# Column sums by whole dense passes, and a fill whose steps stand wider apart, in a one-core decoder layer

## The chip, the cores and the metric

The kernel runs on one core of one Trainium2 chip. The metric is the time of one execution on the device, in microseconds (us), and lower is better. A core has five engines that run side by side, each through its own queue in order: TensorE (PE, matmuls), VectorE (DVE), ScalarE (ACT), GpSimd (POOL) and SyncE (SP), which here mostly issues DMAs. Engines wait for each other by semaphores.

## The reference

One layer of a decoder trunk over 1024 tokens of width 2048, all in float32:

```python
h = rmsnorm(h_res, g_pre)
u = h @ w_in                       # one projection, columns cut into groups
log_a = log_sigmoid(g_lr @ w_a2 + b_a) / GLA_TAU
o_gla = rmsnorm(gla_chunked(gq, gk, gv, log_a), g_head) * silu(g_gate)
o_sb  = stick_breaking(sq, sk, sv) * silu(s_gate)
mix   = concat([o_gla, o_sb]) @ w_out
h_res = h_res + rmsnorm(mix, g_post)
gate  = sigmoid(h_res @ w_g + b_g)
out   = h_res + gate * (p @ w_p)
```

`gla_chunked` is gated linear attention with 4 heads of key width 128. Inside a chunk its score between tokens i and j <= i is the sum over the 128 channels of `q_i * k_j * exp(b_i - b_j)`, where `b` is the running sum of `log_a`. On the diagonal i = j the exponential is 1, so the score is the sum over channels of `q_i * k_i`. `stick_breaking` has 8 heads and plays no part in the change, save that it uses the same buffers afterwards.

## The kernel before, in words

Activations lie with channels on the 128 partitions and tokens along the free dimension, in two halves of 512 tokens. A float32 matrix product is made of three passes: both factors are split into a high part of reduced precision (F32R) and the rest, and `hi*hi`, `lo*hi` and `hi*lo` are accumulated. `split(hi, lo, src)` is one ACT copy and one DVE subtraction.

**First part, the projection and both attentions.** `dense` walks over the projection's units of 128 columns. After every six matmuls (one of 16 slices of the width, both halves, three passes) it calls `step()`, which gives a turn to each of the queues `urgent`, `beside` and `jobs`. Attention is written as generators in `jobs`: a `yield 1` gives the turn back, so that attention's instructions are traced between the dense matmuls. With `RATE_GLA` 1.0 one GLA job gets one turn per step.

`gla` handles a head, half by half. It makes `b` from the gate's matmul `lg` (L414), then `qe` and `ke`, turns the keys by a DMA transpose (`turn_by_dma`, L356 to L362: ACT separates the 16-bit halves into a buffer `mid`, SP issues the transposing DMA into a second one, and DVE joins the halves later, for the keys at L506 in `join_keys`), waits `W0` turns, and then works through seven levels of distance, `LEVELS`. At levels 64 to 2, `factors` makes exponentials and products on DVE and ACT in a buffer `X` (two of them), `level` (L461) makes two matmuls into a PSUM buffer `z` (two of them), and `put` (L455) copies the masked result into the scores `sc` by a `copy_predicated` on DVE. `W1` turns lie ahead of the first level and `W2[i]` ahead of level i.

Two contributions need no matmul between tokens but a sum over channels, that is over partitions: the diagonal (`prep_diag`, `put_diag`) and the last level, distance 1 (`prep_one`, `put_one`). Both go through `by_rows` (L468): four groups of float32 matmuls with a stationary operand of ones, 32 columns wide, each placed in its own quarter of the PE's columns (`tile_position`). So each group writes only those 32 rows of the result that are needed, and four masked copies of 32 rows each follow (L485, L500). The product of the diagonal takes a buffer `E` (two of them), traced right before the first `factors`; `put_diag` stands with the first level.

The values of a head are turned in the same way by `turn` (L364): buffers `X` and `E`, `VW` turns of waiting, then a DVE copy.

**Second part, three products of a recursive form.** The gate, output and last projections are each done by a scheme with sums of quarter matrices, which saves one product in eight. Each stage runs over 8 column blocks j. In most stages a j has one product (24 matmuls); in three stages it has two products, with three weight loads, two weight sums and two splits per j. Sets of activations, split in four pairs of tiles 1024 wide, lie in three slots. While a stage runs, the set for a later stage is made by `fill` (L975) in a free slot: loads into staging buffers (`staged`, three `ar` and one `cw` in turn), for some sets a sum on DVE (`join`), then `to_slot`, which splits. `fill` is a job as well; `RATE_BG` is 0.5, so it gets one turn for every two `step()` calls, and `product` calls `step()` once for every three matmuls, so a stage with 16 products offers 64 turns. After a stage `drain` traces what is left. The change touches the fills that run in two of the long stages: `S3` of the output projection (L1152; two loads and one difference per pair) and `S4` of the last gate (L1341; one load and two sums per pair).

**What sets the order.** The program is traced in the order above, each instruction with its place as its priority; `tc.high_priority(offset=n)` moves it n places ahead. When the kernel is built, a scheduler makes each engine's queue from this: the first in priority among the instructions that it expects to be ready. Weight loads and splits (`ahead`, 700) and the sums behind a product (`soon`, 300) are moved ahead this way; `put_one` has 800 on its copies. On the chip the queues are then fixed.

Of the kernel before, what the change touches and what calls it, by code (L numbers as in the profile page):

```python
# [12 lines left out]
F32R = mybir.dt.float32r  # L13
# [33 lines left out]
RATE_GLA = 1.0  # L47
W0, W1, W2, W4 = 2, 6, (2, 3, 3, 3, 2, 3), 2
RATE_SB = 0.9
W3 = 4  # L50
V_MID, V_END, VW = ("X", "X"), ("E", "E"), 3
L1, L2, PERIOD = 8, 8, 5
# [10 lines left out]
def layer(ctx, tc, xT, w_in, w_gate, w_lr, w_a2, b_a, g_pre, g_head, w_out, g_post,  # L63
# [40 lines left out]
    def f(t):  # L104
        return t.bitcast(F32)
# [196 lines left out]
    with tc.tile_pool(name="att", bufs=1, reuse_waits="tile") as ap:  # L302
# [53 lines left out]
        def turn_by_dma(src, n, mid, tag):  # L356
            pl = at(mid, (P, 2 * n), U16)
            A.activation(pl.rearrange("p (two n) -> p two n", two=2),  # L358
                         src.bitcast(U16)[:, :2 * n].rearrange("p (n two) -> p two n", two=2), AF.Copy)
            tt = at(tag, (P, 2 * n), U16)  # L360
            nc.sync.dma_start(tt.rearrange("p (c t) -> p c t", t=P), pl, transpose=True)
            return tt.rearrange("p (two c t) -> p two c t", two=2, t=P)  # L362

        def turn(vt, dst, parts):  # L364
            w = turn_by_dma(vt, HT, V_MID[parts - 1], V_END[parts - 1])
            for _ in range(VW):
                yield 1
            full = dst if parts == 1 else at("o")
            V.tensor_copy(full.bitcast(U16).rearrange("p (c t two) -> p two c t", c=4, two=2), w)
            if parts == 2:  # L370
                split(*dst, full)
            yield 1
# [31 lines left out]
        def gla(h, kp, qp, vp):  # L404
# [6 lines left out]
            for hf in HALVES:  # L411
# [26 lines left out]
                turned_keys = turn_by_dma(ke, HT, "s", "E")  # L438
                G.tensor_tensor(qe, qe, q, op=ALU.mult)
                for _ in range(W0):  # L440
                    yield 1
# [25 lines left out]

                def by_rows(e, n, m):  # L468
                    z = ps("z")
                    rows = [slice(32 * g, 32 * g + 32) for g in range(4)]  # L470
                    for g, r in enumerate(rows):
                        PE.matmul(z[r, :4 * n].rearrange("p (c t) -> p c t", c=4), f(ones_r)[:, :32],
                                  view(e, n * g, (m, 4), (1, n)), start=True, stop=True,
                                  tile_position=(0, 32 * g))
                    return [(r, z[r, :4 * n]) for r in rows]

                def prep_diag():
                    e = at("E")
                    V.tensor_tensor(e, k, q, op=ALU.mult)
                    return e  # L480

                def put_diag(e):
                    for g, (r, z) in enumerate(by_rows(e, 32, P)):
                        m = mask_s[r, 7 * QT + 32 * g:7 * QT + 32 * g + 32].rearrange("p (c t) -> p c t", c=1)
                        V.copy_predicated(view(sc[r], 32 * g, (P, 4), (1, 32)), m.to_broadcast([32, 4, 32]),  # L485
                                          z.rearrange("p (c t) -> p c t", c=4))

                def prep_one():
                    e = at("E", (P, QT))
                    e4 = e.rearrange("p (s n h) -> p s n h", s=2, h=1)  # L490
                    V.tensor_tensor(e4, queries(b, 1), keys(b, 1), op=ALU.subtract)
                    A.activation(e, e, AF.Exp, scale=1.0 / TAU)
                    times(e4, e4, keys(k, 1))
                    times(e4, e4, queries(q, 1))
                    return e

                def put_one(e):
                    for g, (r, z) in enumerate(by_rows(e, 16, 64)):
                        with tc.high_priority(offset=800):
                            V.copy_predicated(view(sc[r], 32 * g + 1, (QT - 1, 2), (P, 2), (2, 16)),  # L500
                                              view(mask_s[r], 6 * QT + 16 * g, (P, 2), (64, 2), (1, 16)),
                                              z.rearrange("p (s c t) -> p s c t", s=2, c=2))

# [18 lines left out]

                diag, xs = prep_diag(), factors(LEVELS[0])
                for _ in range(W1):
                    yield 1
                for i in range(6):
# [3 lines left out]
                    if i == 0:  # L530
                        ket = join_keys()
                        put_diag(diag)
                    level(i, x)
# [370 lines left out]
    if True:  # L904
# [69 lines left out]

        def fill(name, slot, load, join=None):  # L975
            pairs = []
            ready = load(0)
            yield 1
            for i in range(4):
                now, ready = ready, load(i + 1) if i < 3 else None  # L980
                yield 1
                if join:
                    now = join(*now)
                    yield 1
                pairs.append(to_slot(slot, i, now))
                yield 1
# [164 lines left out]

        job(fill("S3", 0, *both(og_d[1], og_d[0], sub)))  # L1152
        for j in range(8):
# [186 lines left out]
        st_v = state("l")  # L1340
        job(fill("S4", 2, make_4, join_4))  # L1341
        for j in range(8):
# [111 lines left out]
```

## Time and profile before

| | us |
|---|---|
| median of 3 runs | 2054.58 |
| lowest and highest | 2049.41, 2055.2 |
| the profiled execution | 2058.89 |
| its span, first to last instruction | 2057.2 |

Over the span the DMA engines moved 173 GB/s on the mean; the page's 40 slices show 82 to 108 GB/s in most of the first half and 200 to 330 in most of the second. The granted clock of PE stands at 0.9 or more of full speed in each slice. The output stage with two products per j runs from 1433.6 to 1523.7 us of the span, the gate stage with two products per j from 1797.4 to 1888.5; the eight GLA passes lie between about 117 and 548.

To read the rows that follow: a row in order of time has the start, the duration, the engine, the line, the operation with `output<-inputs` by tile names, the shape, and a count where like instructions in a row are put together; brackets give idle time before it and what ended it. Matmuls are pipelined, so a duration is longer than the distance to the next start; what a matmul costs PE is that distance. A row of a list of waits has the waiting instruction, its releaser, then total us, times, and the longest. A row of windows has the stretch, its length, then busy us and count of PE, PEld (weight loads), DVE, ACT and POOL, the granted clock, the DMA share and GB/s. A row of one line's instructions has the shortest, median and longest duration in ns, and the first and last start.

### The profile page before, as it was taken

To read this page: it belongs to the slowest core of one execution; us is meant where nothing else is said; L and a number is where in the kernel's file an instruction comes from. 1 tells how busy PE (TensorE), PEld (TensorE's weight loads), DVE (VectorE), ACT (ScalarE), POOL (GpSimd) and SP (SyncE) were. 2 spreads that over 40 slices of the span, in tenths; PEclk is the share of its full clock that TensorE was granted. 3 is DMA by queue.
4 is the path that set the end of the run, shared out by engine and by line. 5 is a ranking of instruction groups with operands and counts; after the bars stand their busy time and mean duration, and the time that the engine had idled before them with its cause. 6 is when DMAs were issued, how large, how long until landed. Compare 5 with 4: busy or idle time off the path is not lost.

```text
span 2057.2 us, 26551 instructions
## 1 busy us (share of the span) xinstructions
PE 2041.2 (99%) x9632; PEld 1691.3 (82%) x9632; DVE 1466.2 (71%) x2305; ACT 865.9 (42%) x1367; POOL 92.5 (4%) x214
## 2 busy tenths in 40 slices
PE   9999999999999999999999999999999999999998
PEld 7788888888888788888888788888788888878887
DVE  8567777776666676666567677788778778886765
ACT  8333433333455455545457323344233434323332
POOL 0000000000101111101101000000000000000000
PEclk9999999999999999999999999999999999999999
DMA  7122333232244444434335798888888586876762
GB/s 236 53 79 83 89 82 94 82 88 82 86 105 108 96 111 109 115 93 93 79 98 158 262 330 287 310 292 300 315 289 282 167 307 224 301 272 218 235 202 92
DMA packets 237715, 354.90 MB, mean 173 GB/s; under 512 B 132736, under 2 KB 138000, under 8 KB 237584
## 3 DMA queue, kind: packets, MB, share of 16 engines
q1 hardware_dynamic: 236832, 350.97, 53.8%
q10 hardware_dynamic: 720, 2.23, 0.3%
q8 instruction: 75, 1.23, 0.3%
q14 instruction: 56, 0.46, 0.1%
q0 software_dynamic: 32, 0.01, 0.0%
HBM read 249.85 MB, written 73.92 MB: 157 GB/s over the span
## 4 chain that ended last, share of the span: by engine, by line
PE 77%; DVE 10%; DMA 8%; issue 3%; ACT 2%; POOL 0%; SPq 0%; DVEq 0%; POOLq 0%; ACTq 0%
PE dn L102 67%; PE z L102 4%; PE t L102 3%; PE o L102 2%; DVE wl L115 2%; DMA wr<-w_out 1%; DMA ar<-og_d 1%; DVE wr L936 1%; DMA E<-X 1%; DMA wr<-w_g 1%; DMA ar<-h_d 1%; DVE al L115 1%; DMA h_d<-st 1%; DVE ar L933 1%; DVE st L933 0%
## 5 line engine op out<-in xcount | busy, mean ns | idle before, releaser
L102 PE MATMUL dn<-ah,hi 128*128 128x512 f32 x1408 | 558.5, 397 | 1.0 <-ACT ah L271 1.0
L102 PE MATMUL dn<-ah,lo 128*128 128x512 f32 x1408 | 549.4, 390 | 0.0
L102 PE MATMUL dn<-al,hi 128*128 128x512 f32 x1408 | 548.8, 390 | 0.0
L102 PE MATMUL dn<-ah,wl 128*128 128x512 f32 x1216 | 474.4, 390 | 4.0 <-DVE wl L115 3.8
L102 PE MATMUL dn<-ah,wh 128*128 128x512 f32 x1216 | 473.4, 389 | 1.0 <-ACT wh L114 1.0
L102 PE MATMUL dn<-al,wh 128*128 128x512 f32 x1216 | 473.1, 389 | 0.0
L102 PEld LDWEIGHTS dn<-al,hi 128*128 128x128 f32 x1408 | 264.3, 188 | 56.7 <-DVE al L272 0.3
L102 PEld LDWEIGHTS dn<-ah,hi 128*128 128x128 f32 x1408 | 265.0, 188 | 55.0 <-ACT ah L271 3.1
L102 PEld LDWEIGHTS dn<-ah,lo 128*128 128x128 f32 x1408 | 265.1, 188 | 48.5
L114 ACT ACTIVATE wh<-wr 128x1024 fp32r<-128x1024 f32 x152 | 159.7, 1057 | 295.9 <-PE dn L102 221.2
L102 PEld LDWEIGHTS dn<-ah,wl 128*128 128x128 f32 x1216 | 228.3, 188 | 55.1 <-DVE wl L115 7.8
L102 PEld LDWEIGHTS dn<-ah,wh 128*128 128x128 f32 x1216 | 228.3, 188 | 48.8 <-ACT wh L114 2.0
L102 PEld LDWEIGHTS dn<-al,wh 128*128 128x128 f32 x1216 | 228.3, 188 | 47.3
L115 DVE TENSOR_TENSOR wl<-wr,wh 128x1024 fp32r<-128x1024 f32 x152 | 185.1, 1219 | 10.5 <-ACT wh L114 10.3
L114 ACT ACTIVATE hi<-raw 128x512 fp32r<-128x512 f32 x192 | 120.1, 626 | 149.4 <-PE dn L102 146.1
L115 DVE TENSOR_TENSOR lo<-raw,hi 128x512 fp32r<-128x512 f32 x192 | 131.4, 685 | 53.4 <-ACT hi L114 53.1
L358 ACT ACTIVATE X<-E 128x256 uint16<-128x256 uint16 (+2 forms) x96 | 81.1, 844 | 130.7 <-DVE E L640 65.5
L635 DVE TENSOR_TENSOR_SCAN X<-X 128x128 f32<-128x128 f32 (+2 forms) x96 | 98.0, 1021 | 15.7 <-POOL X L629 14.2
L650 DVE COPY v<-E 128x512 uint16<-128x512 uint16 (+1 forms) x160 | 64.3, 429 | 47.3 <-DMA E<-X 44.1
L115 DVE TENSOR_TENSOR s<-v,s 128x512 fp32r<-128x512 f32 (+1 forms) x82 | 52.6, 642 | 61.5 <-ACT s L114 58.2
L936 DVE TENSOR_TENSOR wr<-wr,wr 128x1024 f32<-128x1024 f32 x48 | 58.7, 1222 | 43.7 <-DMA wr<-w_out 21.8
L933 DVE TENSOR_TENSOR wr<-wr,wr 128x1024 f32<-128x1024 f32 x48 | 58.7, 1224 | 41.2 <-DMA wr<-w_g 30.6
(246 smaller groups left out, 2205.8 us busy)
## 6 DMA issues: line engine op xcount, KB each, us to landing
raw<-w_in SPq DMA_DIRECT2D x160, 256.0 KB, 2.6
wr<-w_g SPq DMA_DIRECT2D x64, 512.0 KB, 4.3
wr<-w_out SPq DMA_DIRECT2D x56, 512.0 KB, 4.5
wr<-w_gate SPq DMA_DIRECT2D x40, 512.0 KB, 4.8
g_d<-wr SPq DMA_DIRECT2D x32, 512.0 KB, 3.7
wr<-g_d SPq DMA_DIRECT2D x32, 512.0 KB, 4.9
ar<-h_d SPq DMA_DIRECT2D x28, 512.0 KB, 5.0
ar<-og_d SPq DMA_DIRECT2D x25, 512.0 KB, 5.5
```

The lines of the kernel that those rows point to most:

```text
L102: PE.matmul(o, lhsT, rhs, start=start, stop=stop)
L114: A.activation(hi, src, AF.Copy)
L115: (eng or V).tensor_tensor(lo, src, f(hi), op=ALU.subtract)
L358: A.activation(pl.rearrange("p (two n) -> p two n", two=2), src.bitcast(U16)[:, :2 * n].rearrange("p (n two) -> p two n", two=2), AF.Copy)
L635: V.tensor_tensor_scan(rev, rev, rev, initial=kq[:, n:n + 1], op0=ALU.mult, op1=ALU.bypass)
L650: V.tensor_copy(to[:, :, :m, j], w[:, :, 2 * g:2 * g + m])
L933: V.tensor_tensor(dst, a, b, op=ALU.add)
L936: V.tensor_tensor(dst, a, b, op=ALU.subtract)
```

## The change

There are three edits.

First, the two column sums. `by_rows` is gone. `add_up` sums over all partitions with two full matmuls against the 128x128 ones in F32R, one on the high part and one on the low part of the product: 512 columns wide for the diagonal, 256 for the last level. The products are therefore split: the diagonal's right after its product, in buffers `o`, `o2` and `kt`, ahead of `W0`; the last level's in `X` and `E`. Each sum is followed by one masked copy over all 128 rows instead of four over 32. `put_diag` stands on its own after `W5` = 7 turns, `W1` is 7, and `W2` is shorter by one at the fourth place, so that the turns of a half stay 26 in all. The high priority of `put_one` now covers its matmuls too.

Second, `turn` uses its own destination as the middle buffer when the values are turned for GLA, in place of `X`.

Third, `fill` takes a `pause`. With 1 it is as before. With 4, given for `S3` of the output stage and `S4` of the gate stage, a pair takes 12 turns instead of 3: four, then the next pair's loads, three, then the sum, four, then the split, one.

```diff
-W0, W1, W2, W4 = 2, 6, (2, 3, 3, 3, 2, 3), 2
+W5 = 7
+W0, W1, W2, W4 = 2, 7, (2, 3, 3, 2, 2, 3), 2
...
-            w = turn_by_dma(vt, HT, V_MID[parts - 1], V_END[parts - 1])
+            w = turn_by_dma(vt, HT, dst if parts == 1 else "X", "E")
...
                 G.tensor_tensor(qe, qe, q, op=ALU.mult)
+                diag, pair = at("o"), (at("o2", dt=F32R), at("kt", dt=F32R))
+                V.tensor_tensor(diag, k, q, op=ALU.mult)
+                split(*pair, diag)
                 for _ in range(W0):
                     yield 1
...
-                def by_rows(e, n, m):
+                def add_up(hi, lo):
+                    n = hi.shape[-1]
                     z = ps("z")
-                    rows = [slice(32 * g, 32 * g + 32) for g in range(4)]
-                    for g, r in enumerate(rows):
-                        PE.matmul(z[r, :4 * n].rearrange("p (c t) -> p c t", c=4), f(ones_r)[:, :32],
-                                  view(e, n * g, (m, 4), (1, n)), start=True, stop=True,
-                                  tile_position=(0, 32 * g))
-                    return [(r, z[r, :4 * n]) for r in rows]
+                    mm(z[:, :n], ones_r, hi, True, False)
+                    mm(z[:, :n], ones_r, lo, False, True)
+                    return z
...
+                def put_diag(x):
+                    c4 = "p (c t) -> p c t"
+                    V.copy_predicated(sc.rearrange(c4, c=4),
+                                      mask_s[:, 7 * QT:7 * QT + P].rearrange(c4, c=1).to_broadcast([P, 4, P]),
+                                      add_up(*x).rearrange(c4, c=4))
...
-                    return e
-
-                def put_one(e):
-                    for g, (r, z) in enumerate(by_rows(e, 16, 64)):
-                        with tc.high_priority(offset=800):
-                            V.copy_predicated(view(sc[r], 32 * g + 1, (QT - 1, 2), (P, 2), (2, 16)),
-                                              view(mask_s[r], 6 * QT + 16 * g, (P, 2), (64, 2), (1, 16)),
-                                              z.rearrange("p (s c t) -> p s c t", s=2, c=2))
+                    hi, lo = at("X", (P, QT), F32R), at("E", (P, QT), F32R)
+                    split(hi, lo, e)
+                    return hi, lo
+
+                def put_one(x):
+                    with tc.high_priority(offset=800):
+                        put(6, add_up(*x))
...
-                diag, xs = prep_diag(), factors(LEVELS[0])
-                for _ in range(W1):
+                xs = factors(LEVELS[0])
+                for _ in range(W5):
+                    yield 1
+                put_diag(pair)
+                for _ in range(W1 - W5):
                     yield 1
...
                     if i == 0:
                         ket = join_keys()
-                        put_diag(diag)
...
-        def fill(name, slot, load, join=None):
+        def fill(name, slot, load, join=None, pause=1):
             pairs = []
             ready = load(0)
             yield 1
             for i in range(4):
-                now, ready = ready, load(i + 1) if i < 3 else None
-                yield 1
+                now = ready
+                if pause == 1 and i < 3:
+                    ready = load(i + 1)
+                for _ in range(pause):
+                    yield 1
+                if pause > 1 and i < 3:
+                    ready = load(i + 1)
+                for _ in range(pause - 1):
+                    yield 1
                 if join:
                     now = join(*now)
-                    yield 1
+                    for _ in range(pause):
+                        yield 1
                 pairs.append(to_slot(slot, i, now))
                 yield 1
...
-        job(fill("S3", 0, *both(og_d[1], og_d[0], sub)))
+        job(fill("S3", 0, *both(og_d[1], og_d[0], sub), pause=4))
...
-        job(fill("S4", 2, make_4, join_4))
+        job(fill("S4", 2, make_4, join_4, pause=4))
```

More of the change, by code (lines that the diff above doesn't have):

```diff
@@ L47 @@
 RATE_GLA = 1.0
-W0, W1, W2, W4 = 2, 6, (2, 3, 3, 3, 2, 3), 2
+W5 = 7
+W0, W1, W2, W4 = 2, 7, (2, 3, 3, 2, 2, 3), 2
 RATE_SB = 0.9
 W3 = 4
-V_MID, V_END, VW = ("X", "X"), ("E", "E"), 3
+VW = 3
 L1, L2, PERIOD = 8, 8, 5
@@ L356, in turn_by_dma @@
         def turn_by_dma(src, n, mid, tag):
-            pl = at(mid, (P, 2 * n), U16)
+            pl = at(mid, (P, 2 * n), U16) if isinstance(mid, str) else mid.bitcast(U16)
             A.activation(pl.rearrange("p (two n) -> p two n", two=2),
@@ L466, in level @@
                     put(li, z)
-                def by_rows(e, n, m):
+                def add_up(hi, lo):
+                    n = hi.shape[-1]
                     z = ps("z")
-                    rows = [slice(32 * g, 32 * g + 32) for g in range(4)]
-                    for g, r in enumerate(rows):
-                        PE.matmul(z[r, :4 * n].rearrange("p (c t) -> p c t", c=4), f(ones_r)[:, :32],
-                                  view(e, n * g, (m, 4), (1, n)), start=True, stop=True,
-                                  tile_position=(0, 32 * g))
-                    return [(r, z[r, :4 * n]) for r in rows]
-                def prep_diag():
-                    e = at("E")
-                    V.tensor_tensor(e, k, q, op=ALU.mult)
-                    return e
[L482 to L486, printed above, removed]
+                    mm(z[:, :n], ones_r, hi, True, False)
[6 more added lines that the diff above has]
+                                      add_up(*x).rearrange(c4, c=4))
                 def prep_one():
@@ L494, in prep_one @@
                     times(e4, e4, queries(q, 1))
-                    return e
-                def put_one(e):
-                    for g, (r, z) in enumerate(by_rows(e, 16, 64)):
-                        with tc.high_priority(offset=800):
-                            V.copy_predicated(view(sc[r], 32 * g + 1, (QT - 1, 2), (P, 2), (2, 16)),
-                                              view(mask_s[r], 6 * QT + 16 * g, (P, 2), (64, 2), (1, 16)),
-                                              z.rearrange("p (s c t) -> p s c t", s=2, c=2))
+                    hi, lo = at("X", (P, QT), F32R), at("E", (P, QT), F32R)
[4 more added lines that the diff above has]
+                        put(6, add_up(*x))
                 def join_keys():
```

## The prediction

> **What bounds the kernel now.** I read the page's first part, then the list of what TensorE (PE) waited for, then PE in order of time around the edited groups, then both edited stages as windows.
>
> ```profile
> span 2057.2 us, 26551 instructions
> PE 2041.2 (99%) x9632; PEld 1691.3 (82%) x9632; DVE 1466.2 (71%) x2305; ACT 865.9 (42%) x1367; POOL 92.5 (4%) x214
> ```
>
> ```profile
> PE dn L102 <- DVE wl L115: 3.8, 6, 1.5
> ...
> PE z L472 <- DVE E L479: 1.0, 4, 0.3
> ```
>
> The reader is to see that PE is busy 99% of the span: 16 us of 2057.2 are not. The first wait is for split weights, the second is one of the groups that the change replaces. An edit here can pay only by fewer PE slots or by taking away one of these waits, and it costs wherever it makes PE wait anew. VectorE (DVE) and ScalarE (ACT) have room on average; a stage can still lack it.
>
> **Part 1: column sums in the eight GLA passes (4 heads, 2 halves).** A plain level, seen in PE's order of time (start, duration):
>
> ```profile
> 136.03 0.39 PE L102 MATMUL dn<-al,hi 128*128 128x512 f32 x1
> 136.26 0.60 PE L102 MATMUL z<-X 128*128 128x128 f32 x4
> 136.62 0.48 PE L102 MATMUL dn<-ah,hi 128*128 128x512 f32 x1
> ```
>
> From dense matmul to dense matmul 0.59 us. A level with the diagonal's tiled sum before it (first half of a head), and one with the last level's tiled sum behind it:
>
> ```profile
> 130.91 0.39 PE L102 MATMUL dn<-al,hi 128*128 128x512 f32 x1
> 131.23 0.42 PE L472 MATMUL z<-E,ones_r 128*32 128x128 f32 x8
> 131.59 0.71 PE L102 MATMUL z<-X 128*128 128x128 f32 x4
> 132.06 0.48 PE L102 MATMUL dn<-ah,hi 128*128 128x512 f32 x1
> ```
>
> ```profile
> 153.72 0.39 PE L102 MATMUL dn<-al,hi 128*128 128x512 f32 x1
> 153.95 0.60 PE L102 MATMUL z<-X 128*128 128x128 f32 x4
> 154.49 0.32 PE L472 MATMUL z<-E,ones_r 128*32 128x64 f32 x8
> 154.73 0.50 PE L102 MATMUL dn<-ah,hi 128*128 128x512 f32 x1
> ```
>
> 1.15 and 1.01 us, so the diagonal's sum costs 0.56 and the last level's 0.42, changes of tiling included. In the second half of a head a wait is added:
>
> ```profile
> 182.69 0.39 PE L102 MATMUL dn<-al,hi 128*128 128x512 f32 x1
> 183.33 0.43 PE L472 MATMUL z<-E,ones_r 128*32 128x128 f32 x8 [0.25 <-DVE E L479]
> ```
>
> Here 0.64 us pass between the two starts, against 0.32 above (130.91 to 131.23): 0.32 more, in the four second halves (the four of the list of waits). The new form exists in this trace, as the two passes of the norm's column sum (with the gate's matmul behind), and 256-wide passes as the six of a stick-breaking group:
>
> ```profile
> 168.63 0.39 PE L102 MATMUL z<-X,ones_r 128*128 128x512 f32 x1
> 168.86 0.39 PE L102 MATMUL z<-E,ones_r 128*128 128x512 f32 x1
> 169.09 0.39 PE L102 MATMUL z<-lr,a2c 128*128 128x512 f32 x1
> ```
>
> ```profile
> 602.32 0.88 PE L102 MATMUL t<-s,u 128*128 128x256 f32 x6
> ```
>
> ```profile
> L102 PE MATMUL t<-s,u 128*128 128x256 f32 x288 | 43.7, 283 | 0.8 <-ACT s L114 0.6 <-DVE s L115 0.2
> ```
>
> 0.23 us a pass of 512; of 256 one alone lasts 0.28 and six in a row 0.88, so each further one takes (0.88 - 0.28) / 5 = 0.12. New sums: 2 x 0.23 = 0.46 and 2 x 0.12 = 0.24. PE gains 8 x (0.56 - 0.46) + 8 x (0.42 - 0.24) + 4 x 0.32 = 0.8 + 1.4 + 1.3 = **3.5 us** before new waits.
>
> The Trainium skill (TensorEngine Tiling (Array Packing), Overview, its table of theoretical speedups) speaks against this edit: a stationary operand of at most 32 columns can run up to four times as fast tiled as not. By that, as an estimate, the sums that take 0.36 (131.23 to 131.59) and 0.24 (154.49 to 154.73) tiled would need 1.44 and 0.96 dense. The rows of 168.63 and 168.86 differ: there a sum over 512 columns is done in 0.46.
>
> What the new form adds elsewhere: two splits per pass (one ACT copy, one DVE subtraction each) for eight masked copies that become two.
>
> ```profile
> L485 DVE COPY_PREDICATED s<-mask,z x32: 271/297/311, 133.2 to 506.7; 32x128 f32<-32x128 uint8 x32
> L458 DVE COPY_PREDICATED s<-mask,z x48: 420/440/734, 134.9 to 526.8; 128x256 f32<-128x256 uint8 x48
> L115 DVE TENSOR_TENSOR E<-E,X x8: 682/688/694, 167.0 to 539.9; 128x512 fp32r<-128x512 f32 x8
> ```
>
> ```profile
> 116.00:221.00 105.00, 104.75 (x553) 87.78 (x552) 73.45 (x166) 39.03 (x66) 6.64 (x4) 1.00 0.28 80
> ```
>
> DVE loses 8 x 0.30 = 2.4 us a pass and gets 0.69, about 0.42 (half as wide), 0.44 and at most 2 x 0.44 for the 512-wide copy: 2.4. Even. ACT gets about 1.05 us where it is busy 39.03 of 105 us. Both lie under PE's dense matmuls.
>
> What can hurt is that PE is in order, and a sum now waits for product, ACT copy, DVE subtraction in a row. For the diagonal, in a second half:
>
> ```profile
> 179.88 0.68 DVE L437 TENSOR_TENSOR E<-E,u 128x512 f32<-128x512 f32 x1
> ```
>
> ```profile
> 180.60 1.06 ACT L358 ACTIVATE s<-E 128x1024 uint16<-128x1024 uint16 x1 [0.30 <-DVE E L437]
> ```
>
> ```profile
> 179.11 3.62 POOL L439 TENSOR_TENSOR q<-q,u 128x512 f32<-128x512 f32 x1 [45.80 <-DVE eb L433]
> ```
>
> ```profile
> L479 DVE TENSOR_TENSOR E<-u,u x8: 681/1138/1586, 127.7 to 501.8; 128x512 f32<-128x512 f32 x8
> ```
>
> The product follows L437 (done 180.56), 0.68 us or, overlapped with POOL's multiply as L479 at its longest, 1.59. ACT's copy comes after L358 (181.66), about 0.63; the subtraction 0.69, or again 1.59. Ready at 183.0 to 184.4. The program puts the sum 2 + 7 = 9 steps after the gate's matmul (169.09), a step being six dense matmuls, 1.36 us: 169.32 + 12.3 = 181.6. (Ten steps give 182.9, which is where it stands now.) If PE's queue keeps that place, it waits 1.4 to 2.8 us in each second half, 5.6 to 11 in all. Behind it wait dense matmuls, so all of it counts. But the queue's order is fixed at build time by what is expected to be ready, and the dense matmuls behind are; then only the error of that expectation is left. The nearest measured wait of that kind is the 0.3 of L479. I take 0.2 x 8 = 1.6, range 0 to 11. In first halves the tiled sum stands without such a wait (131.23); the same 0.2 covers them.
>
> The last level's sum now carries the high priority that only its copies had; it can stand ahead of the last level, just when its split is due. Nothing in the trace shows it; bounds 0 and 8 x 0.3 = 2.4, I take 0.1 x 8 = 0.8. Part 1: -3.5 + 1.6 + 0.8 = **-1.1**.
>
> The Trainium skill (GPSIMD Engine Reference, Specifications) says that GpSimd's SBUF interfaces are shared with VectorE and contended by Vector instructions with two SBUF inputs. The longest L479 agrees, and product and subtraction are both of that kind; by it the upper end, 2.8 us, holds wherever POOL still runs.
>
> Small edits at nothing: the turned values use their own destination as the middle buffer, which frees X and adds no instruction; moving levels 0 to 2 by one step leaves the sum of steps at 26; the product in o waits for the store of the half before out of o, which is issued ahead of this half's whole chain up to L437 and lands in 2.2 us:
>
> ```profile
> o_d<-o SPq DMA_DIRECT2D x32, 256.0 KB, 2.2
> ```
>
> If that cover fails, it is the wait above, longer.
>
> **Part 2: the spread fill.** The two stages, and between them a single-load stage as measure:
>
> ```profile
> 1433.60:1523.70 90.10, 88.20 (x385) 71.85 (x384) 67.76 (x66) 27.37 (x29) 0.00 (x0) 1.00 0.87 307
> 1523.70:1567.30 43.60, 43.60 (x194) 36.09 (x194) 33.13 (x37) 15.78 (x16) 0.00 (x0) 1.00 0.80 274
> 1797.40:1888.50 91.10, 88.48 (x386) 71.72 (x385) 65.17 (x67) 24.85 (x26) 0.00 (x0) 1.00 0.71 243
> ```
>
> ```profile
> 1797.00:1815.00 18.00, 16.52 (x73) 13.16 (x72) 16.17 (x19) 6.72 (x8) 0.00 (x0) 1.00 0.81 261
> 1870.00:1888.00 18.00, 18.00 (x81) 14.90 (x80) 9.28 (x9) 5.31 (x5) 0.00 (x0) 1.00 0.49 169
> ```
>
> Sixteen products at 43.60 / 8 = 5.45 us are 87.2; the stages take 2.9 and 3.9 more. So 6.8 us is all that the fill's edit can win. DVE is busy 90% at the head of the second one and 52% at its tail, and PE's loss lies at the head. No instruction is added: 8 and 4 loads, 4 and 8 sums, 4 splits each are the same. They need 49 job turns of the 64 that a stage gives, so the set is ready before its user. In DVE's order of time the harm is visible, a sum of the fill between two weight sums:
>
> ```profile
> 1446.12 1.22 DVE L936 TENSOR_TENSOR wr<-wr,wr 128x1024 f32<-128x1024 f32 x1 [5.21 <-DMA wr<-w_out]
> 1447.33 1.23 DVE L936 TENSOR_TENSOR ar<-ar,cw 128x1024 f32<-128x1024 f32 x1
> ```
>
> Against it: place in the program is not place in time. The next stage's first loads are written after 1523.7, and SP issues them as soon as staging buffers come free:
>
> ```profile
> 1476.23 0.64 SPq L922 DMA_DIRECT2D cw<-og_d  x1
> ```
>
> Loads that the change moves back can be pulled forward in the same way, past the same SP queue, and the weights' instructions already stand ahead of the fill's by their priority. So I take a quarter of 6.8, **-1.7**, nearer to nothing than to all, since the row of 1476.23 shows such a pulling forward and no row shows a load held back by its place; ends +1.5 (one wait more like the longest of the list) and -6.8.
>
> **Sum.** -1.1 - 1.7 = -2.8. The profiled execution took 2058.89 us (its span and 1.7 around it), so 2056.1 on that footing; it lies 4.3 over the median of the runs, 2054.58, and on that footing the forecast is **2051.8**. Differences within 0.3% (6.2 us) are about what a measurement of this kernel can't tell from none.
>
> **Rivals.**
> - The spread takes full effect and the splits come in time: -3.5 - 6.8 + 1.0 (two thirds of one wait of 1.5 left over, my estimate) = -9.3, 2045.3. For it: PE loses time where DVE is fullest. Against: the loads pulled forward. Chance 0.18.
> - The fill doesn't move, because buffers and not the program's place set its time: -1.1 alone, 2053.5. For it: the row of 1476.23. Chance 0.25.
> - Slower: PE keeps the diagonal's sum at step 9 and waits for its split. With the middle of 5.6 to 11: -3.5 + 8.3 + 0.8 - 1.7 = +3.9, 2058.5; with both upper ends and no gain in the fill -3.5 + 11 + 2.4 = +9.9, 2064.5. It decides from waits of 3.5 - 0.8 + 1.7 = 4.4 us in all, that is 1.1 in each second half. For it: ready at 183.0, due at 181.6. Against: the order is made with that in view. Chance 0.14.
> - Dense sums dear: 8 x (1.44 + 0.96 - 0.46 - 0.24) = 13.6 more than reckoned, 2065.3. Against: the rows of 168.63 and 168.86. That is the skill's speed-up rule of TensorEngine Tiling. Chance 0.03.
>
> **Numbers.** The forecast has 0.40. 2045 to 2060 takes in the first two rivals and the lower half of the third, and leaves out the dearest cases. Faster by over 0.3% (below 2048.4): most of the first rival and a little of the forecast, 0.21. Slower by over 0.3% (above 2060.7): the upper part of the third, the fourth, and what I did not see, 0.12. Within: 0.67.
>
> **What would show it.** Right: 0.46 and 0.24 us for the new sums, no L479-like wait over 0.3, DVE's share even over both stages, and stages of 88 to 90 us. Wrong: PE waits of over 1 us for the diagonal's split in second halves; the fill's sums at the same times as now; new waits for weights in the last third of a stage; or a next set late, with PE waiting for it at a stage's start.

## The result, and the profile after

The changed kernel takes 2051.88 us (median of 22 runs, 2048.07 to 2056.65) against 2055.53 us of the kernel before (22 runs beside them, 2049.41 to 2060.89). The ratio is 0.998, with a 95% interval of 0.9975 to 0.9986: 3.7 us, or 0.2%, faster. The forecast was 2051.8. The sum came out; two of its terms did not, and that they cancelled is luck.

The first part of the page of the changed kernel, and the head of its list of what PE waited for:

```profile
span 2054.9 us, 26377 instructions
PE 2037.8 (99%) x9536; PEld 1693.8 (82%) x9536; DVE 1460.8 (71%) x2273; ACT 871.2 (42%) x1383; POOL 94.4 (5%) x214
```

```profile
PE dn L103 <- DVE wl L116: 3.9, 4, 1.5
PE dn L103 <- ACT wh L115: 1.5, 2, 1.0
PE z L103 <- DVE X L154: 1.2, 1, 1.2
```

Ninety-six matmuls are gone (64 tiled ones in each of two sums became 16 each). The four waits for the diagonal's product are gone from the list, and no wait for the new pairs has come in. One new wait, of 1.2 us, is for a buffer `X`. VectorE's share is the same, as reckoned.

PE in order of time, first the end of a first half (the last plain levels and the last level's sum), then a diagonal's sum in a second half:

```profile
153.37 0.39 PE L103 MATMUL dn<-al,hi 128*128 128x512 f32 x1
153.60 0.38 PE L103 MATMUL z<-X 128*128 128x128 f32 x2
153.74 0.36 PE L103 MATMUL z<-X,ones_r 128*128 128x256 f32 x1
153.94 0.28 PE L103 MATMUL z<-E,ones_r 128*128 128x256 f32 x1
154.06 0.38 PE L103 MATMUL z<-X 128*128 128x128 f32 x2
154.19 0.47 PE L103 MATMUL dn<-ah,hi 128*128 128x512 f32 x1
```

```profile
180.58 0.39 PE L103 MATMUL dn<-al,hi 128*128 128x512 f32 x1
180.81 0.39 PE L103 MATMUL z<-o,ones_r 128*128 128x512 f32 x1
181.04 0.39 PE L103 MATMUL z<-kt,ones_r 128*128 128x512 f32 x1
181.26 0.39 PE L103 MATMUL dn<-ah,hi 128*128 128x512 f32 x1
```

From dense matmul to dense matmul the first group takes 0.82 us, where a plain level took 0.59: the last level's sum costs 0.23. It stands between the two matmuls of the level before it, which is its high priority at work. The diagonal's two passes take 0.45 (180.81 to 181.26), with no wait ahead of them.

Where the time went is read best from the gate's matmul, which opens each half:

```profile
117.08 0.39 PE L103 MATMUL z<-lr,a2c 128*128 128x512 f32 x1
168.34 0.39 PE L103 MATMUL z<-lr,a2c 128*128 128x512 f32 x1
```

A first half now takes 51.26 us; before, it took 169.09 - 117.31 = 51.78. The same distances in all the traces (starts of the eight gate matmuls, one execution each; "rest" is from the eighth to the 705th `dn<-ah,hi`, some 94 us later; "between" is from the 1321st `dn<-ah,hi`, at about 1100 us, to the first `dn<-ah,wh`, about 1171 us):

```
us                        first half  second halves        1st to 8th   rest   between
before                    51.77       54.67 55.56 54.66    371.86       93.98  70.45
after                     51.26       53.98 53.98 53.98    367.05       94.82  71.62
e1_fill_only              51.77       54.67 55.22 55.42    372.34       94.00  70.12
e5_sums_only              51.26       54.17 54.07 53.98    367.32       94.54  70.54
e6_turn_only              51.77       54.65 55.57 54.66    371.92       94.00  69.92
e7_sums_without_turn      51.26       54.97 55.55 58.63    374.25       94.42  70.24
e3_diag_only              51.63       55.88 55.29 55.58    373.34       95.20  71.51
e9_diag_turn              51.65       54.83 54.21 54.21    369.83       94.96  74.18
e4_last_only              51.38       54.44 54.40 55.65    371.19       93.76  74.19
e10_last_turn             51.38       54.41 54.39 54.43    370.10       93.80  73.24
```

So the changed kernel gains 4.8 us over seven halves and loses 0.8 in the eighth. The 1.2 that it loses ahead of the second part belongs to this one execution: `e5_sums_only`, whose queues are the same, takes 70.54 there.

### The profile page after: what moved, and what is told of

Its sections match the earlier page's. It is cut to its first block, busy times and chain, and to the rows that moved or that the text cites. A ratio compares the mean times of both kernels' runs of the same rounds, so it can differ in the third digit from the quotient of the medians.

```text
span 2054.9 us, 26377 instructions
## 1 busy us (share of the span) xinstructions
PE 2037.8 (99%) x9536; PEld 1693.8 (82%) x9536; DVE 1460.8 (71%) x2273; ACT 871.2 (42%) x1383; POOL 94.4 (5%) x214
## 4 chain that ended last, share of the span: by engine, by line
PE 44%; DMA 8%; DVE 6%; issue 2%; ACT 1%; SPq 0%; POOL 0%; DVEq 0%; ACTq 0%; POOLq 0%
PE dn L103 40%; PE z L103 2%; DMA wr<-w_out 2%; PE t L103 1%; DVE wl L116 1%; DMA E<-X 1%; DMA wr<-w_g 1%; DMA ar<-og_d 1%; DMA ar<-h_d 1%; DVE wr L934 1%; PE o L103 1%; DVE al L116 1%; DMA h_d<-st 1%; DVE ar L934 0%; ACT wh L115 0%
## 5 line engine op out<-in xcount | busy, mean ns | idle before, releaser
L359 ACT ACTIVATE X<-E 128x256 uint16<-128x256 uint16 (+2 forms) x96 | 81.0, 844 | 146.3 <-DVE E L638 72.0
```

The costliest lines, as they stand in the source:

```text
L359: A.activation(pl.rearrange("p (two n) -> p two n", two=2), src.bitcast(U16)[:, :2 * n].rearrange("p (n two) -> p two n", two=2), AF.Copy)
```

## Experiments

Most kernels take the change apart; each ratio is to the kernel before, in runs beside it, with its 95% interval.

**The fill alone** (`e1_fill_only`): the kernel before with the third edit only.

```diff
-        job(fill("S3", 0, *both(og_d[1], og_d[0], sub)))
+        job(fill("S3", 0, *both(og_d[1], og_d[0], sub), pause=4))
...
-        job(fill("S4", 2, make_4, join_4))
+        job(fill("S4", 2, make_4, join_4, pause=4))
```

> The kernel before with the wider fill steps alone. Theory A (the order of each engine's queue comes from what is ready and from free staging buffers, so the fill does not move): all queues keep the order of before, and the time is that of before within 1 us, ratio 0.9995 to 1.0005; fill sums in the output stage stay 10 us ahead of its start to 27 us into it. Rival B (the gain of 2.0 us that the output stage shows in the trace after is the fill's): 2 us less, ratio 0.999, with the fill's sums spread over some 65 us of the stage.

Measured: 1.0001 (0.9991 to 1.0011), 2054.89 against 2054.64 us. The sums of the fill in VectorE's order of time, second and third pair, in this kernel and then in the changed one:

```profile
1445.72 1.23 DVE L936 TENSOR_TENSOR ar<-ar,cw 128x1024 f32<-128x1024 f32 x1
1452.70 1.22 DVE L936 TENSOR_TENSOR ar<-ar,ar 128x1024 f32<-128x1024 f32 x1
```

```profile
1443.72 1.23 DVE L934 TENSOR_TENSOR ar<-ar,cw 128x1024 f32<-128x1024 f32 x1
1450.43 1.22 DVE L934 TENSOR_TENSOR ar<-ar,ar 128x1024 f32<-128x1024 f32 x1
```

Before, the first of them stood at 1447.33. The two sums are 6.98 and 6.71 us apart; otherwise only the time at which the stage comes differs. Set side by side, the order of instructions on each of the five engines is the same in this kernel as in the kernel before, at every position. The pauses were written into the program and the build took them out again: these loads and sums stand as early as it expected them to run, wherever the program has them.

**The sums alone** (`e5_sums_only`): the changed kernel without the pauses.

```diff
-        job(fill("S3", 0, *both(og_d[1], og_d[0], sub), pause=4))
+        job(fill("S3", 0, *both(og_d[1], og_d[0], sub)))
...
-        job(fill("S4", 2, make_4, join_4, pause=4))
+        job(fill("S4", 2, make_4, join_4))
```

> The changed kernel without the wider fill steps: both dense sums and the turned values' own middle buffer. Every engine's queue stands in the order of the changed kernel's. Theory (all of the change's gain is in the GLA passes): ratio 0.998, as the change. Rival (the fill's edit has a part in it all the same): nearer to 0.999 or above.

Measured: 0.9979 (0.997 to 0.9988), 2051.23 against 2055.57 us. Its queues are those of the changed kernel, and so is its time. All of the gain lies in the first two edits.

**A fill that is really spread** (`e2_spread_by_data`): the changed kernel, where each later load of the two fills is held back by data. A copy of one column into its staging buffer, which the load then overwrites, waits for the latest product's sum `u(j)`.

```diff
             t = mt(*next(spare))
+            if hold[0] is not None:
+                V.tensor_copy(t[:, 0:1], hold[0][:, 0:1])
...
                 if pause > 1 and i < 3:
+                    hold[0] = latest[0]
                     ready = load(i + 1)
+                    hold[0] = None
...
                 add(u(j), p, u(j))
+                latest[0] = u(j)
```

> The changed kernel, with the loads of the two widened fills held back by data: each load behind the first pair's waits for a one-column copy from the latest sum of the stage (9 such copies added). Against the changed kernel, whose time is 0.998 of before. Theory A (the spread was never made, and made it takes the fill out of DVE's fullest stretch): the two stages lose 4 us in place of the 1.1 and 4.6 over 87.0 that they lose in the trace after, so 1 to 3 us less than the changed kernel, ratio to before 0.9965 to 0.9975. Rival C (the waits come from the weights' own loads, and the fill costs nothing where it stands): ratio 0.998 as without it. Rival D (the fill's late loads meet the weights' loads later in the stage): waits for weights move to the last third, ratio 0.9985 or more.

Now the sums of the output stage's fill do stand apart, 16 us from the second pair to the third, where the kernel with the pauses alone has 7.0, and 22 more to the fourth:

```profile
1451.96 1.23 DVE L938 TENSOR_TENSOR ar<-ar,cw 128x1024 f32<-128x1024 f32 x1
1467.96 1.22 DVE L938 TENSOR_TENSOR ar<-ar,ar 128x1024 f32<-128x1024 f32 x1
1490.24 1.22 DVE L938 TENSOR_TENSOR ar<-ar,cw 128x1024 f32<-128x1024 f32 x1
```

Measured: 0.9999 (0.9989 to 1.0009), 2053.91 us, about 0.2% over the changed kernel. PE's waits over both stages and what lies between them, in this kernel:

```profile
PE dn L103 <- DVE wl L116: 2.8, 4, 1.4
```

In the changed kernel that wait has 3.9 us, also four times. So in one execution the spread takes 1.1 us of such waits away, and over the runs it makes the kernel slower: the changed kernel without it has 0.998 (0.9975 to 0.9986), and the two intervals don't meet. The waits for split weights don't come from the fill's place alone. Whether the copies and the later loads cost what was saved wasn't separated. The idea behind the third edit was not fulfilled, and fulfilled in this way it doesn't pay.

**The turn alone** (`e6_turn_only`): the kernel before with the second edit only.

```diff
-            pl = at(mid, (P, 2 * n), U16)
+            pl = at(mid, (P, 2 * n), U16) if isinstance(mid, str) else mid.bitcast(U16)
...
-            w = turn_by_dma(vt, HT, V_MID[parts - 1], V_END[parts - 1])
+            w = turn_by_dma(vt, HT, dst if parts == 1 else "X", "E")
```

> The kernel before with the one edit that a head's turned values use their own destination as the middle buffer. Theory F (the buffer X is what the levels wait for, and this edit frees it): the 0.33 of a level's wait in the trace before goes, at most 0.7 us less, ratio 0.9997 to 1.0000; alone it brings little, since the kernel before has few such waits. Rival G (this edit alone is the gain): ratio 0.998 to 0.999.

Measured: 0.9994 (0.9985 to 1.0003), 2054.27 us. The halves are as before to 0.02 us (the table). Alone, it does nothing that can be measured.

**The sums without the turn** (`e7_sums_without_turn`): the changed kernel with the values' middle buffer back in `X`.

```diff
-            w = turn_by_dma(vt, HT, dst if parts == 1 else "X", "E")
+            w = turn_by_dma(vt, HT, "X", "E")
```

> The changed kernel with the turned values' middle buffer back in X. Theory F: levels wait for X in the second halves as with each sum alone (0.8 to 1.3 us each, four or more times), so 4 to 8 us more than the change, ratio 1.000 to 1.002. Rival H (the waits of the two single-sum runs came from something else, such as the order of the turns): ratio 0.998 as the change, no such waits.

Measured: 1.0014 (1.0005 to 1.0023), 2058.42 us, 0.35% over the kernel with it (0.9979). PE's waits over the eight passes, and one of them in PE's order of time:

```profile
PE z L103 <- DVE X L154: 5.4, 5, 2.8
```

```profile
412.49 0.68 PE L103 MATMUL z<-X 128*128 128x128 f32 x4 [2.78 <-DVE X L154]
```

Ahead of it, in VectorE's order of time:

```profile
409.69 0.43 DVE L452 TENSOR_TENSOR X<-b 128x256 f32<-128x256 f32 x1 [4.04 <-DMA E<-X]
```

The new sums themselves are unharmed (first halves 51.26, as in the changed kernel), but levels wait for their factors. `X` has two buffers, and with the turned values in one of them VectorE can't begin the next `factors` before the transposing DMA has read them. In the four second halves it stands still for this at the same place for 1.89, 1.63, 4.04 and 1.35 us; the 4.04 goes with a transpose that took 5.6 us from issue to landing, where the other three took 3.2 to 3.4. The edit that was costed at nothing decides whether the other one pays. The last level, too, now puts the high part of its split in an `X`, which it didn't before, but the waits don't need that: the diagonal's kernel below has them without it.

**One sum at a time.** Four kernels: the dense diagonal alone (`e3_diag_only`) and with the turn edit (`e9_diag_turn`), the dense last level alone (`e4_last_only`) and with the turn edit (`e10_last_turn`). In the first, at the last level, against the changed kernel (it also lacks the other two edits):

```diff
-                def put_one(x):
-                    with tc.high_priority(offset=800):
-                        put(6, add_up(*x))
+                def put_one(e):
+                    for g, (r, z) in enumerate(by_rows(e, 16, 64)):
...
```

> The kernel before with the dense diagonal sum and its numbers of turns, the last level's sum tiled as before. From the two traces: a tiled diagonal sum costs 0.56 us of PE (0.88 with its wait in second halves), the dense one 0.45. Theory: 8 x 0.11 + 4 x 0.32 = 2.2 us less, ratio 0.9989, no wait at the new sums. Rival (PE waits for the split, the prediction's slower case): waits of over 1 us in second halves and a ratio over 1.000.

> The kernel before with the dense diagonal sum, its numbers of turns, and the turned values in their own middle buffer; the last level's sum tiled. Theory F (X was what the run with the diagonal alone waited for): its waits at levels in second halves go, and 8 x 0.11 + 4 x 0.32 = 2.2 us are saved, less about 1 left where the first stick-breaking head's values still use X: ratio 0.9990 to 0.9995. Rival J (the numbers of turns, or the diagonal's use of other buffers, cause those waits): ratio 1.002 to 1.003 as without the edit.

In the last level's, from the kernel before:

```diff
-                    return e
+                    hi, lo = at("X", (P, QT), F32R), at("E", (P, QT), F32R)
+                    split(hi, lo, e)
+                    return hi, lo
...
+                def put_one(x):
+                    with tc.high_priority(offset=800):
+                        put(6, add_up(*x))
```

> The kernel before with the dense sum of the last level alone, the diagonal's tiled as before. From the traces: a level with the tiled sum behind it costs 0.42 us more than a plain level and some 0.08 in slower matmuls after it; with the dense sum 0.23 more (153.37 to 154.19 against 0.59). Theory: 8 x 0.23 to 0.27 = 1.8 to 2.2 us less, ratio 0.9990. Rival (the small waits taken for the sum's high priority, 0.1 each): 1.0 to 1.4 less, with PE waits listed for the split of E or X.

> The kernel before with the dense sum of the last level and the turned values in their own middle buffer; the diagonal tiled. Theory F: no level waits over 0.5 us, 8 x 0.25 = 2.0 us saved, ratio 0.9988 to 0.9993. Rival J: waits as in the run with the last level's sum alone (two of 1.1 us), ratio 1.001.

Measured, without and with the turn edit: the diagonal 1.003 (1.0019 to 1.004) and 0.9997 (0.9988 to 1.0006); the last level 1.0011 (1.0002 to 1.002) and 1.0002 (0.9989 to 1.0015). What PE waited for in the eight passes, in the diagonal's kernel without the turn edit, and with it:

```profile
PE z L103 <- DVE X L154: 3.4, 4, 1.1
PE o L103 <- DVE s L506: 0.4, 1, 0.4
PE z L103 <- DVE kt L116: 0.3, 1, 0.3
```

```profile
PE z L103 <- DVE X L154: 1.0, 1, 1.0
PE z L103 <- DVE kt L116: 0.3, 1, 0.3
```

Three of the four waits for `X` go with the turn edit. In VectorE's order of time of the kernel without it stands how `X` came late, 2.8 us ahead of PE's first such wait (198.11):

```profile
195.30 0.42 DVE L452 TENSOR_TENSOR X<-b 128x256 f32<-128x256 f32 x1 [1.82 <-DMA E<-X]
```

VectorE stands still until the transposing DMA has read the values out of `X`. PE's four waits stand some 29 us behind the gate's matmul, one in each second half, where `e7_sums_without_turn` has four of its five. Here the last level doesn't use `X`; so what sets them off came with the diagonal (levels that stand a turn later, or a product that no longer takes an `E`), and which of the two it is was not separated. The last level's kernel without the turn edit has one such wait, of 1.0 us.

With the turn edit each sum does gain in the passes: 1.1 and 1.9 us over all eight halves (the table's two columns added), 3.0 together, where both sums in one kernel gain 4.0. (About the quarter that is missing: in the last level's two kernels PE waits once, 0.9 and 1.1 us, for the diagonal's tiled copies, L485, which the dense form doesn't have.) Yet neither kernel is measurably faster than before. In the traces they lose it ahead of the second part, 74.18 and 73.24 us, where the kernel before takes 70.45. The longest of PE's waits there, in the first of them:

```profile
PE dn L103 <- ACT wh L115: 1.8, 2, 1.3
PE t L103 <- ACT s L115: 1.6, 1, 1.6
PE z L103 <- ACT E L633: 1.0, 1, 1.0
```

Nothing of that stretch was edited, and its order is not another one either: set side by side, from 532 us on the order of instructions on each of the five engines is the same in these four kernels as in the kernel before and in the changed one. Only the times at which things come differ there, and one execution of each can't say how much of that comes back in every run. So the medians of the parts measured singly add up to nothing, where both together give 0.2%. In the passes their traces add up to three quarters of it, and why the runs don't show that stays open.

**The sum due earlier** (`e8_sum_due_early`): the changed kernel, the diagonal's sum four turns sooner.

```diff
-W5 = 7
+W5 = 3
```

> The changed kernel with the diagonal's sum due 5 steps after the gate's matmul in place of 9. In the trace of the changed kernel its split is ready 12.0 us after that matmul, and due at 12.5. Rival of the prediction (PE's queue keeps the program's place): the sum stands 30 dense matmuls after the gate's, 7.0 us, and PE waits some 5 us in each second half and 2 in each first, 25 us or more in all, ratio 1.010. Theory (the queue is ordered by what is expected ready): it stands 45 and 48 dense matmuls after it in second halves and 38 and 41 in most first halves, waits of 0 to 1 us each, 0 to 6 in all, ratio 0.998 to 1.001.

Measured: 1.0019 (1.001 to 1.0028), 2061.29 us. PE's waits in the passes, and the sum in a second half:

```profile
PE z L103 <- ACT o L115: 3.9, 7, 0.6
PE z L103 <- DVE kt L116: 2.3, 3, 0.8
```

```profile
179.09 0.50 PE L103 MATMUL z<-o,ones_r 128*128 128x512 f32 x1 [0.61 <-ACT o L115]
180.13 0.39 PE L103 MATMUL z<-kt,ones_r 128*128 128x512 f32 x1
```

Here the rival's mechanism is at work. The waits are far from the four steps of 1.36 us, though. In second halves the sum stands 45 to 48 dense matmuls behind the gate's matmul, where its place in the program is 30: it is put where the build expects the pair to be ready, and from the first head's second half on PE waits for it 0.5 to 0.8 us at a time. At 7 turns the pair is ready in fact, and in the changed kernel no wait is left.

**The last level's sum in its place** (`e11_last_in_place`): the changed kernel without the high priority on the two matmuls.

```diff
+                    z = add_up(*x)
                     with tc.high_priority(offset=800):
-                        put(6, add_up(*x))
+                        put(6, z)
```

> The changed kernel with the last level's sum at its own place in PE's queue, behind both matmuls of the last level, with only its masked copy at high priority. In the changed kernel the sum stands between these two matmuls. Theory: where it stands costs nothing, and it is ready either way: ratio 0.998, the same 0.8 us from dense matmul to dense matmul, and no waits. Rival (the priority wins PE a wait): 0.5 to 2 us more, ratio 0.9985 to 0.999, with waits listed for the split in E.

Measured: 0.9981 (0.9972 to 0.999), 2050.84 us. The same as the changed kernel: the sum's earlier place is neither a gain nor a loss.

**The first stick-breaking turn sooner** (`e12_first_turn_sooner`): the one new wait of the changed kernel stands where GLA hands over to stick-breaking. SyncE's issue, VectorE and PE, in the changed kernel:

```profile
507.00 2.10 SPq L362 DMA_TRANSPOSE E<-X  x1
```

```profile
510.62 0.43 DVE L452 TENSOR_TENSOR X<-b 128x256 f32<-128x256 f32 x1 [1.74 <-DMA E<-X]
```

```profile
513.43 0.68 PE L103 MATMUL z<-X 128*128 128x128 f32 x4 [1.24 <-DVE X L154]
```

The first stick-breaking head's values still use `X` on their way through the transpose; VectorE waits 1.74 us for that DMA, and PE 1.24 us for VectorE. This kernel gives that head's turn one turn of waiting instead of three.

```diff
-                urgent.append(turn(vt, dst[hf], parts))
+                urgent.append(turn(vt, dst[hf], parts, 1 if dst is heads[GLA_HEADS][2] else VW))
...
-        def turn(vt, dst, parts):
+        def turn(vt, dst, parts, vw=VW):
             w = turn_by_dma(vt, HT, dst if parts == 1 else "X", "E")
-            for _ in range(VW):
+            for _ in range(vw):
```

> The changed kernel with one turn of waiting in place of three between the transpose and the copy of the values of the first stick-breaking head, so that its second use of X ends two steps sooner. Only that head's instructions move. Theory F (the wait of 1.2 to 1.4 us at 512 us of the span, at a level of the last GLA half, is for X held by that transpose): the wait goes, 1.1 to 1.4 us less than the change, ratio to before 0.9973 to 0.9975. Rival (the earlier copy waits on DVE for the transpose and holds up what stands behind it): the wait moves to the level before, ratio 0.998 or above.

Measured: 0.9979 (0.997 to 0.9988), 2051.23 us. The wait is still there, at the level before, as the rival had it; VectorE's order of time shows why:

```profile
510.65 0.68 PE L103 MATMUL z<-X 128*128 128x128 f32 x4 [1.63 <-DVE X L154]
```

```profile
508.80 0.74 DVE L370 COPY o<-E 128x1024 uint16<-128x1024 uint16 x1 [1.69 <-DMA E<-X]
```

The earlier copy of the turned values now waits on VectorE for the same transposing DMA, 1.69 us, and the level's products with `X` stand behind it. A middle buffer of their own for these values, or a third `X`, wasn't tried; whether the 1.2 us can be had stays open. No kernel tried here is measurably faster than the change.

## Why the prediction was right, and which of its steps were not

**The new sums' slots: right.** Forecast 0.46 and 0.24 us, measured 0.45 and 0.23. The rows of 168.63 and 168.86 had it, and the rival with dense sums at 1.44 and 0.96 is out. A first half gained 51.77 - 51.26 = 0.51, where 0.10 + 0.18 = 0.28 was reckoned. Added up, the 186 dense matmuls between the two gate matmuls hold PE for 43.22 us before and 42.98 after. Of these 0.24, 0.09 is the slot ahead of the tiled diagonal (130.91 to 131.23, 0.32 in place of 0.23), which was counted; the other 0.15 was not, and that it is an after-effect of the tiled groups is only argued. The 0.08 left over lies in attention's own slots. A second half gained 54.67 - 53.98 = 0.69 against 0.60 reckoned; the 55.56 of the second head had two further small waits.

**The new waits at the sums: mis-sized, 0 instead of +2.4.** This is the term of part 1 that was off. It rested on the product following L437 (the product with the keys, L438 after the change) and its ACT copy following L358 (L359 after). In the changed kernel:

```profile
178.13 0.69 DVE L442 TENSOR_TENSOR o<-u,u 128x512 f32<-128x512 f32 x1
179.06 0.69 DVE L438 TENSOR_TENSOR E<-E,u 128x512 f32<-128x512 f32 x1
179.67 0.68 DVE L116 TENSOR_TENSOR kt<-o,o 128x512 fp32r<-128x512 f32 x1
```

```profile
178.85 0.63 ACT L115 ACTIVATE o<-o 128x512 fp32r<-128x512 f32 x1
```

The product stands ahead of L438, since its factors were there already, and the pair is complete at 180.35, not at 183.0 to 184.4. The sum starts at 180.81. I read the order of the program as the order of the queue, in the same part in which I had said that it is not. The step at which the sum falls was right in kind: 12.47 us after the gate's matmul, where 12.5 (169.09 to 181.6) was worked out. The slower rival needed the pair to be late by 1.1 us; it is early by 0.46. That the rival's mechanism is real shows in `e8_sum_due_early`, where 0.5 to 0.8 us a time came back and made the kernel slower than before.

The product was also feared at 1.59 us where GpSimd works beside it. All eight in the changed kernel, and GpSimd's own product behind the first row above:

```profile
L442 DVE TENSOR_TENSOR o<-u,u x8: 679/684/685, 81.1 to 493.9; 128x512 f32<-128x512 f32 x8
```

```profile
178.37 4.16 POOL L440 TENSOR_TENSOR q<-q,u 128x512 f32<-128x512 f32 x1 [47.57 <-DVE eb L434]
```

None is longer than 0.69. GpSimd's took 4.16 us, where it was 3.62 before, and in its time the subtraction into `kt` took its usual 0.68. By the Trainium skill (GPSIMD Engine Reference, Specifications) VectorE's instructions with two inputs in SBUF contend with GpSimd. The trace agrees, now on one side and now on the other: in three first halves of the changed kernel GpSimd's product takes only 1.6 us, and VectorE's product at L438, which starts 0.3 to 0.4 us after it, takes 1.78 (at 231.03, for one). So the fear was sound, but here it doesn't fall on the pair in second halves.

**"Small edits at nothing": wrong for one of them.** That the turned values use another middle buffer "frees X and adds no instruction" was true, and its price alone is nothing (0.9994). But the rest of the change makes the levels need `X` while the transposing DMA still reads it, and I didn't follow who holds that buffer, and when, before and after. Without the edit the sums make the kernel slower (1.0014), with it faster (0.9979): 0.35% between them, 7 us. In the table it is 374.25 - 367.32 = 6.9 us over the first seven halves: its waits for `X` there (4.6) and, by estimate, 1.7 by the slow clock behind the longest of them (last section).

**The fill: 0 instead of -1.7.** The second rival held in this term, and so did the sign of being wrong that was named for it, the fill's sums at the same times as before. Its place in the program doesn't set its time (`e1_fill_only`) and its data can (`e2_spread_by_data`); that the staging buffers do was not tested by itself. The row of 1476.23, a load pulled forward into the stage before, was in view, and even so a quarter of the effect was kept. As the builder puts instructions forward whenever they can run, the pauses had nothing to hold them with. The two stages now:

```profile
1432.80:1521.00 88.20, 87.42 (x386) 72.02 (x385) 66.23 (x64) 25.67 (x26) 0.00 (x0) 1.00 0.84 303
1794.70:1886.30 91.60, 88.37 (x386) 71.73 (x385) 65.07 (x67) 24.44 (x25) 0.00 (x0) 1.00 0.71 240
```

88.2 and 91.6 against 90.1 and 91.1: this looks like 1.4 us of the 1.7, and isn't. With the same order on each engine, the difference is that between two executions.

**The sum.** Forecast: -1.1 for the sums and -1.7 for the fill, -2.8. By the traces the passes give -4.0 (-4.8 over seven halves, +0.8 in the last, with its wait of 1.24), the fill 0; the medians differ by 3.7. Single executions scatter too much to close the account to a few tenths: the span of the profiled one fell by 2.3 only, since ahead of the second part it lost 1.2, and behind that a slow clock cost it 1.7 by estimate (below), against the 1.4 of the two stages.

## What to carry to other kernels

Where a builder orders the queues by readiness, a pause in the program can change nothing at all (the fill), while another changes a queue and costs time (`W5` = 3): look at the queues of the built kernel before costing such an edit, and hold work back by data if it must be held. Where an edit moves work that uses a buffer with only two copies, list who holds it before and after, and for how long a DMA keeps it; freeing it can be worth more than the instructions saved. And parts measured singly needn't add up to the whole: test an edit by taking it out of the whole as well as by putting it in alone.

## What the runs showed of the hardware

The granted clock of PE can halve for 3.4 us behind waits of one to three us. First the changed kernel (waits of 1.0 and 0.5 us, the last ending at 1170.04), then `e7_sums_without_turn` (2.78), then the stretch ahead of such a fall in `e4_last_only` (1.6), and at the end one without a fall, in `e9_diag_turn` (1.6). The columns are the stretch, its length, then busy us and count of PE, PEld, DVE, ACT and POOL, granted clock, DMA share, GB/s:

```profile
1168.01:1171.42 3.41, 1.92 (x7) 1.23 (x7) 3.41 (x4) 1.98 (x2) 0.00 (x0) 1.00 0.78 320
1171.42:1174.83 3.41, 3.41 (x9) 2.64 (x8) 2.48 (x4) 0.00 (x0) 0.00 (x0) 0.50 0.86 252
```

```profile
410.11:413.52 3.41, 1.03 (x9) 1.06 (x10) 3.41 (x10) 0.71 (x2) 0.00 (x0) 1.00 0.19 49
413.52:416.94 3.42, 3.42 (x12) 2.84 (x12) 2.95 (x8) 0.91 (x2) 0.00 (x0) 0.50 0.27 104
```

```profile
1133.62:1137.03 3.41, 1.67 (x9) 1.38 (x10) 1.88 (x5) 2.54 (x5) 0.00 (x0) 1.00 0.90 251
```

```profile
1130.59:1134.00 3.41, 1.78 (x8) 1.03 (x6) 1.80 (x3) 2.19 (x4) 0.00 (x0) 1.00 0.90 269
```

Each fall lasts 3.41 us at half clock. If PE does half its work in that time, it loses 1.7 us, an estimate; the wait of 2.78 then cost 4.5 in all, and the 74.19 of `e4_last_only` in the table holds 1.7 of this kind. By the traces' records of the clock, the three falls come 1167.36, 406.19 and 1129.81 us after the clock's first rise, which is 342, 119 and 331 times 3.413 us. So they stand on a grid of that step, wherever the wait is, and the stretches above are steps of it. That can be why like waits differ: in the same stretch of the program, with the same queues, PE waits 1.6 us in `e4_last_only`, `e9_diag_turn` and `e10_last_turn`, and 1.7 in `e8_sum_due_early`, and only the first of them falls.

In the step ahead of a fall PE was busy for 1.92, 1.03 and 1.67 us. The Trainium skill (TensorE: Matmul & The Clock Gate, Part 1: The HAM clock gate) gives a window of 3413 ns for this gate and has the clock fall after an idle window of about 3.4 us. The length agrees. The condition doesn't: in none of these steps was PE idle throughout. Nor is it the busy time of the step alone, as the profile counts it: 1.78 passed without a fall, and at the end of `e9_diag_turn` even 1.50. What exactly the limit is was not settled.
